# Plain f32 projections in place of three split products, and expert slots opened in the front

## The chip, the cores and the metric

The kernel runs on one core of one Trainium2 chip. The metric is the device time of one execution in microseconds, and the median of several executions is compared. The profile is one execution taken by the hardware profiler.

## The reference

One layer of a streaming encoder for 256 frames of width 2048, all in f32. A projection of the normalised input feeds two mixers of 1024 channels each, a gated causal convolution and an RWKV-7 recurrence; their joined output is projected back and added. A mixture of 32 experts (one of four groups, then two of its eight experts for each token) and a last norm follow.

```python
def reference(x, norm_mix, w_in, ..., norm_final):
    h = x
    for l in range(DEPTH):                      # DEPTH = 1
        u = rms_norm(h, norm_mix[l])
        proj = u @ w_in[l]                      # 2048 -> 2*1024 + 3*1024 + 288
        conv_val = proj[..., :D_CONV]
        conv_gate = proj[..., D_CONV:2 * D_CONV]
        rwkv_cols = proj[..., 2 * D_CONV:]
        y_conv = conformer_conv(conv_val, conv_gate, conv_dw[l], ...)
        y_rwkv = rwkv7_time_mix(rwkv_cols, shift_mu[l], ...)
        mixed = jnp.concatenate([y_conv, y_rwkv], axis=-1)
        h = h + mixed @ w_out[l]                # 2048 -> 2048
        v = rms_norm(h, norm_ffn[l])
        h = h + hierarchical_moe(v, router_group_w[l], ..., expert_w_down[l])
    return rms_norm(h, norm_final)
```

An expert is `(silu(v @ w_gate) * (v @ w_up)) @ w_down` with 2048 x 512, 2048 x 512 and 512 x 2048 weights. The expert weights are 403 MB of the 471 MB that the core moves.

## The kernel before

All is on one core, and activations stay in SBUF. Until the experts, they are held with channels on the 128 partitions and the 256 tokens along the free axis, so the tokens are the moving operand of a projection and a 128 x 128 piece of the weights the stationary one.

**Input norm (`norm_in`, L278).** The input is scaled by the norm's gain into xn, TensorE forms the LoRA columns of the projection (`w_lo`, 288 wide, L315) and the sum of squares from it, and the reciprocal root is spread over a PSUM bank `rstd`. Then y = xn * rstd is formed in eight parts and split in two: yh is the value rounded to the matmul type fp32r, written by ScalarE, and yl the rest, written by VectorE.

**Projections (`proj`, L251).** A block has 256 output columns, in two halves of 128. Its weights come by SyncE's queue in chunks of 8 x 128 rows (1 MB) into the ring of pool `ringA`, whose six slots of 8 KB a partition hold the input (two slots) and weight chunks (four). `split` (L242) makes from every four rows of 128 a high part on ScalarE and a low part on VectorE. The product is the sum of three fp32r matmuls for each 128 rows: w_h x_h, w_h x_l and w_l x_h (L273 to L275). `w_in` has 20 blocks over 16 x 128 rows. `w_out` has eight blocks, done in a pass over the first six RWKV row groups, a pass over the eight convolution row groups, and a remainder over the last two (`rest_block`, L789).

**The front's order (`front`, L712).** Convolution and RWKV "duos" alternate, each with two pairs of heads or two channel groups: c0 r0 c1 r1 c2 r2 c3, the LayerNorm, r3. An RWKV duo needs its K, R and V blocks in that order (`rwkv_duo`), and its own chain of small matmuls (`rwkv_mats`, `rwkv_inv`, `rwkv_out`) runs between the projection matmuls at a set priority. Weight loads and splits have a high priority. The order on each engine is written when the program is built, from priorities.

**Experts.** They run in pairs, 16 of them, each with 24 chunks of 1 MB. `expert_up` and `expert_down` take the weights as the moving operand in plain f32, and gate, up and down products of the two experts of a pair run side by side on the two column halves of TensorE. Chunks go round a ring of 21 slots: NA = 6 in ringA, NB = 6 in ringB (opened when RWKV's tiles are closed), ND = 3 in ringD (opened after the split room is closed), NEX = 1 in ringE, and five tiles of the pool `yp` that hold yh, yl and mix in the front. `ORDER` sets the sequence. Two more places are lent once from the accumulator's tile, as the chunks from number LENT on. `fetch` (L1092) issues the load on SyncE's queue, which executes in order and waits where a slot is not yet free.

Of the kernel before, what the change touches and what calls it, by code (L numbers as in the profile page):

```python
# [21 lines left out]
D = 2048  # L22
# [16 lines left out]
WSLOT = {4: "ylb", 5: "yla", 6: 0, 7: 1}  # L39
RING = 1024  # L40
NA, NB, ND, NEX = 6, 6, 3, 1
# [5 lines left out]
LENT = 13  # L47


def ORDER(A, B, C, D, E):  # L50
    return C[0:3] + B + A[0:2] + C[3:] + D + A[2:4] + E + A[4:]

# [12 lines left out]


class Parts:
    def __init__(self, tiles, n):
        self.tiles, self.n = tiles, n

    def __getitem__(self, k):
        n = self.n
        if isinstance(k, slice):
            return self.tiles[k.start // n][:, k.start % n:(k.stop - 1) % n + 1]
        return self.tiles[k // n][:, k % n]


class Block:
# [163 lines left out]
    def split(self, view):  # L242
        nc = self.nc
        hi = self.spl.tile([128, 4, 256], F32R, tag="hi", name="hi")
        lo = self.spl.tile([128, 4, 256], F32R, tag="lo", name="lo")
        hi, lo = (t[:, 0:view.shape[1], 0:view.shape[2]] for t in (hi, lo))
        nc.scalar.activation(hi, view, AF.Copy)  # L247
        nc.vector.tensor_sub(lo, view, hi.bitcast(F32))  # L248
        return hi, lo

    def proj(self, rows, k0, nk, xh, xl, x0, slot=None):  # L251
        cols = (0, 128)
        accs = [self.bank(self.pacc, [128, 256], "acc") for _ in cols]
        early, self.early = self.early, []
        for b in range(0, nk, 8):
            nb = min(8, nk - b)
            if not early:
                with self.tc.high_priority(offset=2000):
                    c = self.chunk(rows[:, k0 + b:k0 + b + nb], slot)
            for g in range(0, nb, 4):  # L260
                ng = min(4, nb - g)
                with self.tc.high_priority(offset=2000):
                    if early:
                        c, cut = early.pop(0)
                    else:
                        cut = None
                    hi, lo = cut or self.split(c[:, g:g + ng, :])
                for ci, cc in enumerate(cols):
                    for j in range(ng):
                        kt = b + g + j  # L270
                        w_h, w_l = hi[:, j, cc:cc + 128], lo[:, j, cc:cc + 128]
                        x_h, x_l = (x[x0 + kt] for x in (xh, xl))
                        self.mm(accs[ci], w_h, x_h, start=kt == 0, stop=False)  # L273
                        self.mm(accs[ci], w_h, x_l, start=False, stop=False)
                        self.mm(accs[ci], w_l, x_h, start=False, stop=kt == nk - 1)  # L275
        return accs

    def norm_in(self):  # L278
# [13 lines left out]
        xn = [self.rwkv_parts(i, F32, "y") for i in range(2)]  # L292
# [3 lines left out]
        for g in range(4):  # L296
            sq = self.spl.tile([128, 4, 256], F32, tag="hi" if g % 2 else "lo", name="nsq")
            A.activation(sq, x(4 * g, 4), AF.Square)
            for k in range(4 * g, 4 * g + 4):
                o, c = xn[k // 8][k % 8], self.nmix_s[:, k:k + 1]  # L300
# [19 lines left out]
        for step in PSTART:  # L320
            n = int(step[1:] or 0)
            for i in range(2):
                ts = slice(128 * i, 128 * i + 128)
                if step[0] == "l":
                    ordered(la[i], xn[n // 8][n % 8][:, ts], wl[n], start=n == 0, stop=n == 15)
# [3 lines left out]
                else:  # L329
# [5 lines left out]
        yh, yl = (Parts([self.ypool.tile([128, 8, 256], F32R, tag=n + h, name=n + h) for h in "ab"], 8)  # L335
                  for n in ("yh", "yl"))
        tmp = self.ypool.tile([128, 4, 2, 256], F32, tag="mix", name="ytmp")
        first = [self.chunk(self.w_in[DC // 256][:, 8 * b:8 * b + 8]) for b in range(2)]
        self.early = []
        for g in range(8):  # L340
            s = slice(2 * g, 2 * g + 2)
# [4 lines left out]
            if g % 2:  # L346
                c = first[g // 4]
                k = 2 * (g - 1) % 8
                self.early.append((c, self.split(c[:, k:k + 4]) if g < 6 else None))
        self.yh, self.yl = yh, yl  # L350
        self.la, self.rs = la, rs

    def rwkv_parts(self, i, dt, name):
        return Parts([self.mp.tile([128, n, 256], dt, tag=f"m{i}{h}", name=f"{name}{i}{h}")
                      for h, n in (("a", 6), ("b", 2))], 6)

    def w_in_cols(self, c0):
        return self.proj(self.w_in[c0 // 256], 0, 16, self.yh, self.yl, 0)

    def shift(self, ps, mu, omu, out):  # L360
        nc = self.nc
        nc.scalar.activation(out, ps, AF.Copy, scale=omu)
        nc.vector.scalar_tensor_tensor(out[:, 1:256], ps[:, 0:255], mu, out[:, 1:256],
                                       op0=OP.mult, op1=OP.add)

# [57 lines left out]
    def rwkv_k(self, s, kps):  # L423
# [4 lines left out]
        self.shift(kps, self.pcol("mu_k", p), self.omu[:, 1, p:p + 1], ks)  # L428
# [23 lines left out]
        s.update(AR=AR, bt=bt, kt=kt, ks=ks)  # L452

# [122 lines left out]
    def rwkv_out(self, s):  # L576
# [63 lines left out]
        V.tensor_mul(ys, ys, g)  # L640
        self.hilo(ys, self.mr[0][p], self.mr[1][p])
        self.tap(f"mix{p}", ys)
# [18 lines left out]
    def conv_norm(self):  # L661
# [11 lines left out]
        rstd = self.ypool.tile([128, 256], F32, tag="yha", name="lnr")  # L673
        A.activation(rstd, var, AF.Sqrt, bias=self.c_ln, scale=1.0 / DC)
        V.reciprocal(rstd, rstd)
        for j in range(8):
            c = self.mix[:, j]
            V.tensor_mul(c, c, rstd)
# [4 lines left out]

    def hilo(self, src, hi, lo):
        self.nc.scalar.activation(hi, src, AF.Copy)
        self.nc.vector.tensor_sub(lo, src, hi.bitcast(F32))
# [25 lines left out]
    def front(self):  # L712
        tc, nc = self.tc, self.nc
        self.mix = self.ypool.tile([128, 8, 256], F32, tag="mix", name="mix")
        self.mr = [self.rwkv_parts(i, F32R, "mr") for i in range(2)]
        V = nc.vector
        with tc.issue_after(self.gate_y.ins), tc.issue_after(self.gate_h.ins):
# [20 lines left out]
    def mix_out(self):  # L738
        m = self.ap.tile([128, 2, 8, 256], F32R, tag="vt", name="m")
        self.mh, self.ml = ([m[:, i, j] for j in range(8)] for i in range(2))  # L740
        self.w_out_pass(8, 6, *self.mr, 0)
        for j in range(8):
            self.hilo(self.mix[:, j], self.mh[j], self.ml[j])
        self.tap("mix", self.mix)
        self.w_out_pass(0, 8, self.mh, self.ml, 0, WSLOT)
# [29 lines left out]
    def w_out_pass(self, k0, nk, xh, xl, x0, slots={}):  # L775
        for b in range(8):
            ps = self.proj(self.w_out[b], k0, nk, xh, xl, x0, slots.get(b))
# [11 lines left out]
    def rest_block(self, b):  # L789
        accs = [self.bank(self.pacc, [128, 256], "acc") for _ in range(2)]  # L790
        cs = slice(256 * b, 256 * b + 256)
        hi, lo = (t[:, b % 3] for t in self.wsp)
        with self.tc.high_priority(offset=2000):
            for k in range(2):
                self.nc.scalar.activation(hi[:, k], self.wrest[k][:, cs], AF.Copy)
                self.nc.vector.tensor_sub(lo[:, k], self.wrest[k][:, cs], hi[:, k].bitcast(F32))
        for i in range(2):
# [497 lines left out]
```

## Time and profile before

| | |
|---|---|
| median of 3 runs | 1467.24 us (1467.2 to 1469.68) |
| profiled execution, its own time | 1469.49 us |
| its span | 1467.7 us |
| TensorE busy | 1399.4 us (95%), 8738 matmul records |
| VectorE busy | 648.2 us (44%) |
| ScalarE busy | 415.5 us (28%) |
| moved by DMA | 471.48 MB, mean 321 GB/s |
| granted TensorE clock, mean | 0.989 |

In the profile PE is TensorE's matmuls, PEld its weight loads, DVE VectorE, ACT ScalarE, POOL GpSimd, SP SyncE, and SPq SyncE's queue. A plain f32 matmul leaves two matmul records, an fp32r one leaves one; both are printed as f32. Matmuls overlap in the pipeline, so the step from one record's start to the next one's is their cost, not the duration of one, and a busy PE can still have slack. L219 is the line of the helper `mm`, which issues most matmuls; they are told apart by the names of their operands, out<-in: acc is a projection's accumulator, g and u the experts' gate and up products, y their down product, gt the gathering of tokens, mm the RWKV chain.

### The profile page before, as it was taken

The page shows a single profiled execution, that of the slowest core. Times are in us where ns is not written, and L with a number is a line of the kernel's source. Part 1 is how long each engine was busy: PE and PEld are TensorE (multiplying, and loading weights), DVE is VectorE, ACT ScalarE, POOL GpSimd, SP SyncE. Part 2 cuts the span into 40 slices and gives each one's busy share as a digit, 9 for nine tenths or more (in the row PEclk, how much of TensorE's full clock was granted, in tenths as well). Part 3 has the DMA queues.
Part 4 walks back from the last instruction along what each step waited for, and adds up shares of the span by engine and source line. Part 5 has one row for each costly group of instructions (what it writes and reads, how often), then busy time and mean ns, then how long its engine had stood idle before and what let it go on. Part 6 is the DMA issues. An engine that isn't in the chain of part 4 may idle for free.

```text
span 1467.7 us, 21322 instructions
## 1 busy us (share of the span) xinstructions
PE 1399.4 (95%) x8738; PEld 854.7 (58%) x8738; DVE 648.2 (44%) x1323; ACT 415.5 (28%) x770; POOL 34.3 (2%) x66
## 2 busy tenths in 40 slices
PE   8999999999999979999999999999999998999995
PEld 6989988888899944344344344344344343443432
DVE  6996977968867432232232232232132221312313
ACT  6657666676695420000000000000010000000103
POOL 5000000000000000000000000000000000000000
PEclk9999999999999989999999999999999999999997
DMA  8442432422548777999999999999999999999994
GB/s 300 158 149 96 142 119 90 152 96 89 180 138 333 301 273 324 424 423 427 424 424 425 424 424 423 426 424 424 425 424 424 424 425 424 423 427 424 423 422 151
DMA packets 68678, 471.48 MB, mean 321 GB/s; under 512 B 7984, under 2 KB 10096, under 8 KB 13280
## 3 DMA queue, kind: packets, MB, share of 16 engines
q1 hardware_dynamic: 67344, 467.96, 78.5%
q0 software_dynamic: 1088, 2.09, 0.6%
q8 instruction: 71, 1.16, 0.3%
q14 instruction: 31, 0.25, 0.0%
q10 hardware_dynamic: 144, 0.01, 0.0%
HBM read 467.93 MB, written 2.10 MB: 320 GB/s over the span
## 4 chain that ended last, share of the span: by engine, by line
PE 58%; DMA 26%; DVE 12%; ACT 3%; issue 1%; SPq 0%; ACTq 0%; DVEq 0%
DMA w<-in_w_up_dram 18%; PE acc L219 12%; PE y L219 10%; PE g L219 9%; PE u L219 9%; DMA w<-in_w_down_dram 8%; PE mm L219 7%; PE gt L219 6%; DVE lo L248 3%; PE cb L219 3%; DVE mix L659 2%; DVE MB L496 1%; PE acc L315 1%; ACT hi L247 1%; PE cn L219 1%
## 5 line engine op out<-in xcount | busy, mean ns | idle before, releaser
L219 PE MATMUL u<-w,xe 128*64 128x512 f32 x1016 | 244.1, 593 | 10.3 <-DMA w<-in_w_up_dram 10.2
L219 PE MATMUL g<-w,xe 128*64 128x512 f32 x1016 | 241.4, 597 | 10.4 <-DMA w<-in_w_gate_dram 7.9
L219 PE MATMUL y<-w,hT 128*64 128x512 f32 (+1 forms) x1040 | 232.2, 594 | 0.7 <-ACT hT L1038 0.7
L1056 DVE TENSOR_TENSOR acc<-acc,cb 128x512 f32<-128x512 f32 (+1 forms) x122 | 80.9, 674 | 208.4 <-PE cb L219 208.4
L219 PEld LDWEIGHTS u<-w,xe 128*64 128x64 f32 x1016 | 76.1, 137 | 159.8 <-issue 136.1
L1030 DVE TENSOR_TENSOR hid<-sg,u 128x256 f32<-128x256 f32 x32 | 19.7, 614 | 319.0 <-PE u L219 319.0
L219 PEld LDWEIGHTS g<-w,xe 128*64 128x64 f32 x1016 | 71.8, 137 | 148.4 <-issue 127.6
L219 PEld LDWEIGHTS y<-w,hT 128*64 128x64 f32 x1040 | 70.6, 137 | 134.1 <-issue 118.1
L248 DVE TENSOR_TENSOR lo<-w,hi 128x1024 fp32r<-128x1024 f32 x108 | 127.6, 1182 | 39.8 <-ACT hi L247 27.1
L1026 ACT ACTIVATE sg<-g 128x512 f32<-128x512 f32 x16 | 9.6, 597 | 462.2 <-PE g L219 462.2
L219 PE MATMUL gt<-S,vt 128*128 128x128 f32 x1024 | 127.8, 282 | 6.7 <-DVE xe L977 5.2
L219 PEld LDWEIGHTS gt<-S,vt 128*128 128x128 f32 x1024 | 122.4, 196 | 15.7 <-DVE xe L977 8.7
L247 ACT ACTIVATE hi<-w 128x1024 fp32r<-128x1024 f32 x108 | 110.6, 1025 | 43.6 <-PE acc L219 40.4
L1069 ACT ACTIVATE yh<-y,gate 128x512 fp32r<-128x512 f32 (+1 forms) x65 | 44.3, 682 | 250.4 <-PE y L219 250.4
L659 DVE SCALAR_TENSOR_TENSOR mix<-UP,dw_s,mix 128x256 f32<-128x256 f32 x240 | 104.1, 479 | 2.8 <-ACT mix L657 2.5
L219 PE MATMUL acc<-yha,hi 128*128 128x256 f32 x320 | 91.6, 286 | 1.1 <-ACT sg L646 0.6
L219 PE MATMUL acc<-yhb,lo 128*128 128x256 f32 x320 | 92.0, 287 | 0.0
L219 PE MATMUL acc<-yla,hi 128*128 128x256 f32 x320 | 91.7, 287 | 0.0
L219 PE MATMUL acc<-ylb,hi 128*128 128x256 f32 x320 | 91.3, 285 | 0.0
L219 PE MATMUL acc<-yha,lo 128*128 128x256 f32 x320 | 90.9, 285 | 0.0
L219 PE MATMUL acc<-yhb,hi 128*128 128x256 f32 x320 | 90.4, 282 | 0.0
L977 DVE TENSOR_TENSOR xe<-gt,nffnp_s 128x512 f32<-128x512 f32 (+1 forms) x65 | 44.4, 684 | 88.8 <-PE gt L219 88.8
(356 smaller groups left out, 1913.3 us busy)
## 6 DMA issues: line engine op xcount, KB each, us to landing
w<-in_w_gate_dram SPq DMA_DIRECT2D x127, 1024.0 KB, 19.6
w<-in_w_up_dram SPq DMA_DIRECT2D x127, 1024.0 KB, 19.6
w<-in_w_down_dram SPq DMA_DIRECT2D x126, 1024.0 KB, 19.6
w<-in_w_in_dram SPq DMA_DIRECT2D x40, 1024.0 KB, 5.0
w<-in_w_out_dram SPq DMA_DIRECT2D x8, 768.0 KB, 4.4
w<-in_w_out_dram SPq DMA_DIRECT2D x6, 1024.0 KB, 5.1
xT_s<-in_xT_dram SPq DMA_DIRECT2D x4, 512.0 KB, 6.5
wlast<-in_w_out_dram SPq DMA_DIRECT2D x2, 1024.0 KB, 6.9
```

Of the source, the lines that this page charges most:

```text
L219: self.nc.tensor.matmul(*a, **k)
L247: nc.scalar.activation(hi, view, AF.Copy)
L248: nc.vector.tensor_sub(lo, view, hi.bitcast(F32))
L315: m = nc.tensor.matmul(*a, **k)
L496: V.copy_predicated(MB[:, 2 * h + c], self.mkP.rearrange("p a b -> p (a b)"), P12[h])
L659: V.scalar_tensor_tensor(c, u, d, c, op0=OP.mult, op1=OP.add)
L977: self.nc.vector.tensor_mul(xe[:, a:a + n], ps, self.nffnp_s[:, k0:k0 + n, None].to_broadcast([128, n, 128]))
L1026: A.activation(sg, gp, AF.Silu)
L1030: V.tensor_mul(hid, *(t.rearrange("s (p f) -> s f p", f=4)[:, f:f + 2] for t in (sg, up)))
L1056: V.tensor_add(self.acc[:, i, c0:c0 + w], (self.vt if first else self.acc)[:, i, c0:c0 + w], cb)
L1069: A.activation(yh, yp, AF.Copy, scale=gate)
```

## The change

`proj` takes the activations and the weights as they are: one plain f32 matmul for each 128 rows in place of three fp32r ones. With that `split`, `hilo`, `Parts` and the low tiles go; y is formed in place in xn, in the tiles yha and yhb; the norm's squares lie in yla and ylb; the mixers' outputs are read as they are (mr and mix). `conv_norm` keeps its reciprocal root in PSUM. The room of the splits, pool `spl`, is gone, and ring D gets four slots (ring E goes) and is opened at the very start. The expert ring begins with yla, ylb and ring D. The first six expert fetches wait, by a semaphore, for the K shift of duos 0, 1 and 2, two each. The second w_out pass takes the ring for blocks 4 and 5 instead of yla and ylb.

```diff
-WSLOT = {4: "ylb", 5: "yla", 6: 0, 7: 1}
+WSLOT = {6: 0, 7: 1}
-NA, NB, ND, NEX = 6, 6, 3, 1
+NA, NB, ND = 6, 6, 4
+EARLY = 6
-LENT = 13
-def ORDER(A, B, C, D, E):
-    return C[0:3] + B + A[0:2] + C[3:] + D + A[2:4] + E + A[4:]
+LENT = 14
+def ORDER(A, B, C, D):
+    return C[0:2] + D + C[2:4] + B + C[4:] + A
...
+    def proj(self, rows, k0, nk, x, x0, slot=None):
...
-            for g in range(0, nb, 4):
...
-                for ci, cc in enumerate(cols):
-                    for j in range(ng):
-                        kt = b + g + j
-                        w_h, w_l = hi[:, j, cc:cc + 128], lo[:, j, cc:cc + 128]
-                        x_h, x_l = (x[x0 + kt] for x in (xh, xl))
-                        self.mm(accs[ci], w_h, x_h, start=kt == 0, stop=False)
-                        self.mm(accs[ci], w_h, x_l, start=False, stop=False)
-                        self.mm(accs[ci], w_l, x_h, start=False, stop=kt == nk - 1)
+            for ci, cc in enumerate(cols):
+                for j in range(nb):
+                    self.mm(accs[ci], c[:, j, cc:cc + 128], x[x0 + b + j], start=b + j == 0, stop=b + j == nk - 1)
...
-        xn = [self.rwkv_parts(i, F32, "y") for i in range(2)]
+        xn = [self.ypool.tile([128, 8, 256], F32, tag=t, name="y") for t in ("yha", "yhb")]
+        sqt = [self.ypool.tile([128, 2, 4, 256], F32, tag=t, name="nsq") for t in ("yla", "ylb")]
...
-            y = tmp[:, g % 4]
-            V.tensor_mul(y, xn[g // 4][2 * (g % 4):2 * (g % 4) + 2], rstd[:, None, :].to_broadcast([128, 2, 256]))
-            self.gate_h = A.activation(yh[s], y, AF.Copy)
-            self.gate_y = V.tensor_sub(yl[s], y, yh[s].bitcast(F32))
...
+            y = xn[g // 4][:, 2 * (g % 4):2 * (g % 4) + 2]
+            self.gate_y = V.tensor_mul(y, y, rstd[:, None, :].to_broadcast([128, 2, 256]))
+        self.y = [xn[k // 8][:, k % 8] for k in range(16)]
...
-        rstd = self.ypool.tile([128, 256], F32, tag="yha", name="lnr")
-        A.activation(rstd, var, AF.Sqrt, bias=self.c_ln, scale=1.0 / DC)
-        V.reciprocal(rstd, rstd)
+        A.activation(var, var, AF.Sqrt, bias=self.c_ln, scale=1.0 / DC)
+        V.reciprocal(var, var)
...
         for i in range(2):
-            self.rwkv_k(ss[i], ps[i])
+            gate = self.rwkv_k(ss[i], ps[i])
+        if len(self.gates) < EARLY:
+            self.gates += [gate] * 2
...
-                for w, x in ((hi, 0), (hi, 1), (lo, 0)):
-                    self.mm(accs[i], w[:, k, c], self.mr[x][6 + k], ...)
+                self.mm(accs[i], self.wrest[k][:, c:c + 128], self.mr[:, 6 + k], start=k == 0, stop=k == 1)
...
+        gate = self.gates.pop(0) if self.gates else None
+        return self.fetch(self.slot(rings, "w"), which, e, q, gate)
...
-        self.nc.sync.dma_start(v, src)
+        d = self.nc.sync.dma_start(v, src)
+        if gate is not None:
+            self.after(d, gate)
...
             self.ring = E(P("ringA", NA))
+            rd = E(P("ringD", 1))
...
-                    sp = fw.enter_context(ExitStack())
-                    self.spl = sp.enter_context(P("spl", 3, "right"))
...
-                    C = [(self.ypool, n) for n in ("yhb", "yha", "mix", "ylb", "yla")]
+                    C = [(self.ypool, n) for n in ("yla", "ylb", "yha", "yhb", "mix")]
```

## Rows read from the trace of the kernel before

**Rows 1.** Table by stretches: length, each engine's busy us, clock, DMA share, GB/s.

```profile
27.00:447.00 420.00, 407.17 (x3558) 372.58 (x3558) 349.18 (x705) 288.51 (x549) 21.68 (x42) 1.00 0.39 132
447.00:519.00 72.00, 72.00 (x615) 71.92 (x614) 42.57 (x79) 33.65 (x63) 0.00 (x0) 1.00 0.84 331
526.00:592.00 66.00, 62.71 (x323) 30.55 (x323) 17.00 (x50) 5.54 (x9) 0.00 (x0) 0.96 0.75 302
592.00:977.00 385.00, 382.57 (x1947) 168.37 (x1946) 99.44 (x197) 27.62 (x42) 0.00 (x0) 1.00 1.01 424
977.00:1391.00 414.00, 393.26 (x1948) 170.35 (x1946) 99.94 (x198) 27.68 (x43) 0.52 (x1) 1.00 1.01 424
```

**Rows 2.** Waits of TensorE, 27 to 447 us: total us, times, longest.

```profile
PE mm L219 <- DVE DT L498: 6.9, 8, 1.4
PE mm L219 <- ACT sq L430: 2.5, 5, 1.0
PE mm L219 <- ACT EP L536: 0.9, 5, 0.3
PE acc L219 <- ACT sg L646: 0.6, 1, 0.6
PE acc L219 <- DVE ks L363: 0.5, 2, 0.3
```

**Rows 3.** The chain of waits, expert stage: start us, us, what.

```profile
592.15 3.58 PE g L219 x16
...
647.16 3.58 PE g L219 x16
...
985.47 19.70 DMA w<-in_w_up_dram
1005.23 21.31 DMA w<-in_w_down_dram
1026.61 19.58 DMA w<-in_w_up_dram
```

**Rows 4.** Waits of TensorE, 526 us to the end: total us, times, longest.

```profile
PE u L219 <- DMA w<-in_w_up_dram: 10.2, 8, 1.3
PE g L219 <- DMA w<-in_w_gate_dram: 7.9, 7, 1.4
```

**Rows 5.** Timeline and waits, SyncE's queue and TensorE, the experts' beginning.

```profile
376.53 0.42 SPq L1095 DMA_DIRECT2D w<-in_w_gate_dram  x1
...
517.11 2.98 SPq L1095 DMA_DIRECT2D w<-in_w_down_dram  x3
...
526.05 3.75 PE L219 MATMUL gt<-S,vt 128*128 128x128 f32 x16 [0.98 <-DVE S L948]
...
533.99 0.33 SPq L1095 DMA_DIRECT2D w<-in_w_down_dram  x1
...
SPq L1095 <- PE g L219: 19.4, 2, 13.9
```

**Rows 6.** Plain f32 products: timeline, its group (mean ns), the chain of waits.

```profile
19.55 5.98 PE L315 MATMUL acc<-w,y1a 128*128 128x288 f32 x24
...
L315 PE MATMUL acc<-w,y1a 128*128 128x288 f32 x24 | 6.0, 406 | 0.0
...
378.33 1.73 PE cn L219 x8
```

**Rows 7.** Split products in the chain of waits: start us, us, what.

```profile
29.12 9.07 PE acc L219 x80
...
447.67 53.09 PE acc L219 x448
```

**Rows 8.** One of six groups of w_in's split products, by form.

```profile
L219 PE MATMUL acc<-yha,hi 128*128 128x256 f32 x320 | 91.6, 286 | 1.1 <-ACT sg L646 0.6 <-DVE ks L363 0.5
```

**Rows 9.** The splits' groups: busy us, mean ns, idle before and its cause.

```profile
L248 DVE TENSOR_TENSOR lo<-w,hi 128x1024 fp32r<-128x1024 f32 x108 | 127.6, 1182 | 39.8 <-ACT hi L247 27.1 <-PE acc L219 9.2 <-PE mm L219 3.3
L247 ACT ACTIVATE hi<-w 128x1024 fp32r<-128x1024 f32 x108 | 110.6, 1025 | 43.6 <-PE acc L219 40.4 <-issue 1.5 <-ACT bv L465 0.7
```

**Rows 10.** Timeline of TensorE around a piece of RWKV's chain.

```profile
300.84 0.39 PE L219 MATMUL mm<-dd,at 128*128 128x128 f16 x4
301.04 0.36 PE L219 MATMUL acc<-yha,hi 128*128 128x256 f32 x1
301.24 0.28 PE L219 MATMUL acc<-yla,hi 128*128 128x256 f32 x1
301.36 0.28 PE L219 MATMUL acc<-yha,lo 128*128 128x256 f32 x1
```

**Rows 11.** Loads of w_in (KB, us to landing), and SyncE's wait.

```profile
w<-in_w_in_dram SPq DMA_DIRECT2D x40, 1024.0 KB, 5.0
...
SPq L239 <- DVE lo L248: 250.4, 29, 13.6
```

More of the change, by code (lines that the diff above doesn't have):

```diff
@@ L240, in chunk @@
         return v
[L242 to L251, printed above, removed]
+    def proj(self, rows, k0, nk, x, x0, slot=None):
         cols = (0, 128)
@@ L334, in norm_in @@
                     ordered(rstd[:, ts], self.ones, dg[:, i], start=True, stop=True)
[L335 to L339, printed above, removed]
-        for g in range(8):
-            s = slice(2 * g, 2 * g + 2)
-            y = tmp[:, g % 4]
-            V.tensor_mul(y, xn[g // 4][2 * (g % 4):2 * (g % 4) + 2], rstd[:, None, :].to_broadcast([128, 2, 256]))
-            self.gate_h = A.activation(yh[s], y, AF.Copy)
-            self.gate_y = V.tensor_sub(yl[s], y, yh[s].bitcast(F32))
[L346 to L350, printed above, removed]
+        self.early = [self.chunk(self.w_in[DC // 256][:, 8 * b:8 * b + 8]) for b in range(2)]
+        for g in range(8):
+            y = xn[g // 4][:, 2 * (g % 4):2 * (g % 4) + 2]
+            self.gate_y = V.tensor_mul(y, y, rstd[:, None, :].to_broadcast([128, 2, 256]))
+        self.y = [xn[k // 8][:, k % 8] for k in range(16)]
         self.la, self.rs = la, rs
-    def rwkv_parts(self, i, dt, name):
-        return Parts([self.mp.tile([128, n, 256], dt, tag=f"m{i}{h}", name=f"{name}{i}{h}")
-                      for h, n in (("a", 6), ("b", 2))], 6)
     def w_in_cols(self, c0):
-        return self.proj(self.w_in[c0 // 256], 0, 16, self.yh, self.yl, 0)
+        return self.proj(self.w_in[c0 // 256], 0, 16, self.y, 0)
     def shift(self, ps, mu, omu, out):
         nc = self.nc
-        nc.scalar.activation(out, ps, AF.Copy, scale=omu)
+        a = nc.scalar.activation(out, ps, AF.Copy, scale=omu)
         nc.vector.scalar_tensor_tensor(out[:, 1:256], ps[:, 0:255], mu, out[:, 1:256],
                                        op0=OP.mult, op1=OP.add)
+        return a
     def tt(self, name, shape=(128, 256), dt=F32):
@@ L427, in rwkv_k @@
         ks = self.lg("ks")
-        self.shift(kps, self.pcol("mu_k", p), self.omu[:, 1, p:p + 1], ks)
+        gate = self.shift(kps, self.pcol("mu_k", p), self.omu[:, 1, p:p + 1], ks)
         sq = self.tt("sq")
@@ L452, in rwkv_k @@
         s.update(AR=AR, bt=bt, kt=kt, ks=ks)
+        return gate
     def rwkv_r(self, s, rps):
@@ L714, in front @@
         self.mix = self.ypool.tile([128, 8, 256], F32, tag="mix", name="mix")
-        self.mr = [self.rwkv_parts(i, F32R, "mr") for i in range(2)]
+        self.mr = self.mp.tile([128, 8, 256], F32, name="mr")
         V = nc.vector
-        with tc.issue_after(self.gate_y.ins), tc.issue_after(self.gate_h.ins):
+        with tc.issue_after(self.gate_y.ins):
             V.tensor_copy(self.id16[:, 0], self.ident)
@@ L738, in mix_out @@
     def mix_out(self):
[L739 to L743, printed above, removed]
+        self.w_out_pass(8, 6, [self.mr[:, j] for j in range(8)], 0)
         self.tap("mix", self.mix)
-        self.w_out_pass(0, 8, self.mh, self.ml, 0, WSLOT)
+        self.w_out_pass(0, 8, [self.mix[:, j] for j in range(8)], 0, WSLOT)
         with self.tc.high_priority(offset=2000):
@@ L773, in conv_duo, with w_out_pass @@
             self.conv_taps((2 * d, 2 * d + 1), ps, sg)
[L775 removed]
+    def w_out_pass(self, k0, nk, x, x0, slots={}):
         for b in range(8):
[L777 removed]
+            ps = self.proj(self.w_out[b], k0, nk, x, x0, slots.get(b))
             for i in range(2):
@@ L790, in rest_block @@
         accs = [self.bank(self.pacc, [128, 256], "acc") for _ in range(2)]
[L791 to L793 removed]
+        for i in range(2):
+            c = 256 * b + 128 * i
             for k in range(2):
[L795 to L802 removed]
+                self.mm(accs[i], self.wrest[k][:, c:c + 128], self.mr[:, 6 + k], start=k == 0, stop=k == 1)
         return accs
@@ L807, in w_out_rest @@
         V, A = nc.vector, nc.scalar
-        self.wsp = [self.mp.tile([128, 3, 2, 256], F32R, tag=t, name=t) for t in ("m0a", "m1a")]
         self.vt = self.ap.tile([128, 2, D], F32, tag="vt", name="vt")
@@ L1084, in expert_chunk @@
             return self.fetch(self.lent.pop(0), which, e, q)
-        return self.fetch(self.slot(rings, "w"), which, e, q)
+        gate = self.gates.pop(0) if self.gates else None
+        return self.fetch(self.slot(rings, "w"), which, e, q, gate)
     def slot(self, rings, name):
@@ L1090, in slot, with fetch @@
         return pool.tile([128, 2048], F32, tag=tag, name=name)
-    def fetch(self, c, which, e, q):
+    def fetch(self, c, which, e, q, gate=None):
         src = self.wsrc(which, e, q)
         v = c[:, 0:4 * src.shape[2]].rearrange("p (a b) -> p a b", a=4)
-        self.nc.sync.dma_start(v, src)
+        d = self.nc.sync.dma_start(v, src)
+        if gate is not None:
+            self.after(d, gate)
         return v
```

46 lines of the change are left out of this document (11 added, 35 removed).

## The prediction, made before the changed kernel was built or run

> **What bounds the kernel now.** I read the table by stretches first [rows 1]. Three numbers decide in it: how much of a stretch TensorE is without a matmul, what the DMA engines move, and the granted clock. [...] From 592 us the DMA moves 424 GB/s without a break. VectorE is the second busiest in the front, 349 of 420 us, but TensorE waits for other engines 6.9, 2.5, 0.9, 0.6 and 0.5 us there, 11.4 us in all [rows 2]. So the front is TensorE's.
>
> The expert stage has two laws, which the chain of waits shows [rows 3]. From 592 us it is made of matmuls, and a pair of experts takes 647.16 - 592.15 = 55.0 us. From 985 us it is made of DMA landings of about 19.7 us, three to a pair, 59 us: TensorE consumes faster than weights come, and the store that it started with is used up. TensorE's waits for weights are 10.2 and 7.9 us, in small pieces [rows 4].
>
> The third view, decisive for the freed room, is SyncE's queue [rows 5]. The kernel has 21 slots for expert weights and two lent ones. The first fetch leaves at 376.53 us, the 23rd in the group that begins at 517.11 us, before the experts' first gather at 526.05 us. The 24th stands at 533.99 us: it waited 13.9 us, until a first expert matmul had freed a slot. So the experts start with all 23 places filled or asked for, and the DMA idles after that for want of room (302 GB/s from 526 to 592 us [rows 1]), not because it began late.
>
> **The change part by part.** All sums are made against the profiled execution: 1469.49 us, span 1467.7, 2.25 us over the median of 1467.24.
>
> *One plain product for three.* A plain f32 call leaves two matmul records: the twelve calls of the LoRA product on the six parts of y1a are 24 records, of 288 columns, and take 5.98 us; less the last record's own 0.41, that is 5.57 / 23 = 242 ns from record to record, and 256/288 of it is 215 ns. The mean product of the convolution norm, 256 columns wide, gives the same: 8 records in 1.73 us, 216 each [rows 6]. A plain projection matmul thus costs 2 x 215.5 = 431 ns. The stationary operand changes from call to call in the LoRA rows too, so its loads are in that figure.
>
> A split product is one record. 80 in a row take 9.07 us, 113.4 ns each; 448 in a row 53.09 us, 118.5 ns each [rows 7]. Three are 340 to 356 ns. The new form is therefore dearer on TensorE by 75 to 91 ns for each triple.
>
> How many: w_in has 20 column blocks x 16 x 2 = 640 calls ([rows 8]: 320 records for each of six products, 1920 = 3 x 640). The first pass of w_out has 8 x 6 x 2 = 96, the second 128, the remainder 32. The 736 of the first two run in the 27-447 stretch, where both paces occur; I take 115 ns, or 345 a triple: 736 x 86 = 63.3 us. The 160 others run at the slower pace: 160 x 75.5 = 12.1 us. Sum +75.4 us. With 113.4 ns for the 736 it is 736 x 90.8 + 12.1 = 78.9; with 118.5 for all it is 67.6.
>
> *What TensorE gets back.* First, waits. ScalarE loses 108 copies of 1025 ns, VectorE 108 subtractions of 1182 ns [rows 9], some 239 us of work on the two engines that RWKV's chain runs on. None of it is on the path by itself: TensorE was kept busy beside it. It can return at most the 12.8 us in which TensorE lacked a matmul. Second, restarts. After a piece of the RWKV chain the second split product starts 0.20 us after the first, against 0.12 between the next ones [rows 10]. Such steps number about 150 in the front, so at most 150 x 0.085 = 12.8 us goes with them; part of it is no loss, since the first product starts early, and plain products follow f32 or f16 work at their own pace in the rows of 256 columns. The bounds are 0 and 26 us. I take 15: longer projection matmuls and idler helpers cover more of the chain, but the order on TensorE is written at build time and will keep some waits.
>
> *Start and norms.* y is now formed in place, so its later parts wait for the LoRA products that read the unscaled values. These end about when the first projection starts anyway, and that one needs the first half only. The LayerNorm scale stays in PSUM: a few operations of under 2 us. The remainder of w_out loses its own splits; TensorE is full there. Together 0, within 2 us.
>
> *Slots in the front.* Four ring-D slots and the two former low-part tiles, yla and ylb, are open from the start or from the end of the input norm; six fetches are gated on the K shifts of duos 0 to 2. yha and yhb follow the last input projection. Eight chunks of 1.049 MB, 2.47 us each at 424 GB/s, move out of the stretch 447-526. But the number of slots stays 21 plus two, all were asked for before the experts began [rows 5], and from there a chunk is fetched when one is consumed, as before. A store of the same size carries TensorE equally far, to its 985 us. Gain 0; between 0 and -8 x 2.47 = -20 us if the store was in truth short. It delays nothing visible: the w_in loads land in 5.0 us, and four ring slots hold two column blocks, 2 x 32 x 0.431 = 27.6 us of matmuls.
>
> *Sum.* 75.4 - 15 + 0 = +60 us, all before the experts start (526 to about 586 us); everything behind is shifted whole. 1469.5 + 60 = 1529.5 for a profile, 1527 for the median. Bounds of the terms: 67.6 - 26 = +42, and 78.9 - 0 = +79, that is 1509 to 1546.
>
> **The rivals.**
>
> *A. The early slots pay.* If the expert stage's DMA limit is set by when fetching starts, eight chunks count: 1527 - 20 = 1507. For it: from 985 us landings are the chain [rows 3]. Against: the fetch at 533.99 waited for a matmul, not for the DMA [rows 5], and the pairs from 592 us are made of matmuls alone [rows 3].
>
> *B. The gated fetches block SyncE's queue.* A fetch that waits for ScalarE's K shift (L428) holds every w_in load queued behind it, and TensorE starves once the 27.6 us of stored blocks less the 5.0 of a landing are gone, 22.6 us. SyncE's queue is indeed one that blocks: it waited 250.4 us for the splits' subtractions in the front [rows 11]. The price of a gate passed 10 us after that cover is 10 us, once in each of three duos: 1557. Against: a gate belongs to the block that runs just before the loads behind it.
>
> *C. Faster: a record of plain f32 streams once.* If one record took a single stream of 256 columns, as a split product does, a call would cost 2 x 113.4 = 227 ns instead of 345. The place is the front's TensorE, and it decides from under 345 ns a call. 736 x 118 + 160 x 128 = 107 us less, 1360 us, if the RWKV chain on VectorE (349 us, less some 130 of splits) can follow. Against it stand the 242 and 216 ns [rows 6]; nothing in the trace is for it. [...]
>
> *D. The front is VectorE's, so the splits were the price.* Then the front would shrink with 128 us less there. TensorE's 407.2 of 420 us rules it out beyond the 12.8 us already counted.
>
> **How the numbers follow.** Forecast (1512 to 1546 around 1527): 0.75. A: 0.07. B and other new waits of TensorE: 0.13. C: 0.03. The remaining 0.02 is a cancellation that I can't name. The range holds the forecast, A, and B up to about half of its price: 1506 to 1552. A change under 0.2%, 3 us, can't be told from none for this kernel; the only cases that end faster are C and half of the unnamed, 0.03, same 0.01, slower 0.96.
>
> **What would show it.** Right: products acc of 1792 records at 215 to 216 ns from record to record; first expert matmul near 586 us with expert weights landed long before; pairs of 55 us, then landings of 19.7 us in threes; DMA rate in the front up by the early chunks and nothing gained for it. SyncE's first fetch that waits on an expert matmul shows that the slots were full again. A is right if the part from the first gather to the end is shorter than before's 1467.7 - 526 = 942 us by ten or more. B is right if TensorE waits for w_in landings. C is right if records stand 110 ns apart. Wrong altogether if TensorE's waits in the front grow, or if the first gather comes before 560 us.

## The result, and the profile of the changed kernel

The changed kernel takes 1546.64 us (median; 1545.65 to 1548.09) where the kernel before took 1467.22 in four runs: 1.054 times as long [1.0523, 1.0561]. The forecast was 1527 with a range of 1506 to 1552. The direction and most of the size are right; 20 us are not in the sum.

The profiled execution took 1546.83 us, 77.3 more than that of before. One event divides the difference: the experts' first gather starts at 600.00 us in place of 526.05 [rows 5]. So 73.95 us arise ahead of it, 3.4 behind it.

The table by stretches of the changed kernel follows. Columns are start:end, length, busy us of TensorE, its weight loads, VectorE, ScalarE and GpSimd, then granted clock, DMA share and GB/s. The last line is a stretch of the landing-bound part.

```profile
27.00:447.00 420.00, 414.97 (x2569) 338.92 (x2568) 226.12 (x552) 173.36 (x373) 15.85 (x35) 1.00 0.38 128
447.00:519.00 72.00, 62.34 (x322) 49.79 (x320) 21.82 (x51) 25.66 (x60) 0.00 (x0) 0.91 0.35 124
600.00:666.00 66.00, 62.76 (x323) 30.52 (x323) 16.82 (x50) 5.54 (x9) 0.00 (x0) 0.96 0.74 301
666.00:1051.00 385.00, 382.58 (x1946) 168.19 (x1945) 99.36 (x196) 27.35 (x42) 0.00 (x0) 1.00 1.01 422
1095.00:1435.00 340.00, 320.72 (x1570) 136.53 (x1566) 80.68 (x158) 22.50 (x34) 0.51 (x1) 1.00 1.01 422
```

Beside [rows 1]: from 27 to 447 us VectorE has 123 us less to do and ScalarE 115, and TensorE is as full as it was, lacking a matmul for 5.0 us instead of 420.00 - 407.17 = 12.8. The second line is the surprise. In the same stretch before, TensorE was full; here 9.7 of 72 us have no matmul, and the granted clock is 0.91, a mean over the two values that this trace has, 1.00 and 0.50 (1.00 from 487 to 491 us, 0.50 from 514 to 516.4). In the expert stage the rate is 422 GB/s where it was 424 and, in the landing-bound part of before, 425.

The products themselves, from the chain of waits of the changed kernel (start us, us, what):

```profile
94.58 7.83 PE acc L209 x36
...
721.35 3.58 PE g L209 x16
...
776.41 3.58 PE g L209 x16
...
1061.63 19.58 DMA w<-in_w_up_dram
1081.28 21.22 DMA w<-in_w_down_dram
```

Thirty-six records in a row take 7.83 us; less the last one's own 0.38 (as long as its group's mean below), that is 7.45 / 35 = 213 ns from start to start. A pair of experts still takes 776.41 - 721.35 = 55.1 us, and from 1062 us the chain is landings of 19.6 and 21.2 us, as in [rows 3].

### The profile page after: what moved, and what is told of

It reads as the page before. It is cut to its first block, busy times and chain, and to the rows that moved or that the text cites. A ratio compares the mean times of both kernels' runs of the same rounds, so it can differ in the third digit from the quotient of the medians.

```text
span 1545.0 us, 19057 instructions
## 1 busy us (share of the span) xinstructions
PE 1472.1 (95%) x7842; PEld 864.8 (56%) x7842; DVE 513.6 (33%) x1171; ACT 300.0 (19%) x617; POOL 29.0 (2%) x66
## 4 chain that ended last, share of the span: by engine, by line
PE 60%; DMA 25%; DVE 13%; ACT 1%; issue 1%; SPq 0%; DVEq 0%; ACTq 0%
DMA w<-in_w_up_dram 17%; PE acc L209 16%; PE y L209 9%; PE g L209 8%; PE u L209 8%; DMA w<-in_w_down_dram 8%; PE mm L209 7%; DVE mix L616 6%; PE gt L209 5%; PE cb L209 3%; DVE MB L454 1%; PE acc L286 1%; PE cn L209 1%; DVE xe L918 1%; DMA w<-in_w_lo_dram 0%
## 5 line engine op out<-in xcount | busy, mean ns | idle before, releaser
L209 PE MATMUL acc<-y,w 128*128 128x256 f32 x1280 | 303.8, 384 | 0.0
L209 PEld LDWEIGHTS acc<-y,w 128*128 128x128 f32 x1280 | 234.9, 190 | 35.5 <-issue 7.4
L209 PE MATMUL u<-w,xe 128*64 128x512 f32 x1008 | 240.8, 593 | 13.0 <-DMA w<-in_w_up_dram 13.0
L971 DVE TENSOR_TENSOR hid<-sg,u 128x256 f32<-128x256 f32 x32 | 19.6, 612 | 322.1 <-PE u L209 322.1
L1011 DVE SCALAR_TENSOR_TENSOR yl<-y,gate,yh 128x512 fp32r<-128x512 f32 (+1 forms) x65 | 48.0, 738 | 62.1 <-ACT yh L1010 62.1
L209 PE MATMUL acc<-mr,w 128*128 128x256 f32 x256 | 63.3, 386 | 0.0
L209 PE MATMUL cb<-yh,ST 128*128 128x512 f32 (+1 forms) x130 | 57.8, 445 | 0.4 <-DVE acc L997 0.4
L209 PEld LDWEIGHTS cb<-yh,ST 128*128 128x128 f32 x130 | 24.3, 187 | 54.5 <-issue 51.1
L209 PE MATMUL cb<-yl,ST 128*128 128x512 f32 (+1 forms) x130 | 51.2, 395 | 0.3 <-DVE yl L1011 0.3
L209 PE MATMUL acc<-mix,w 128*128 128x256 f32 x192 | 44.5, 395 | 6.7 <-DVE mix L638 6.7
## 6 DMA issues: line engine op xcount, KB each, us to landing
w<-in_w_gate_dram SPq DMA_DIRECT2D x128, 1024.0 KB, 19.7
w<-in_w_up_dram SPq DMA_DIRECT2D x126, 1024.0 KB, 19.7
w<-in_w_down_dram SPq DMA_DIRECT2D x126, 1024.0 KB, 19.6
```

The lines of the kernel that those rows point to most:

```text
L209: self.nc.tensor.matmul(*a, **k)
L971: V.tensor_mul(hid, *(t.rearrange("s (p f) -> s f p", f=4)[:, f:f + 2] for t in (sg, up)))
L1011: V.scalar_tensor_tensor(yl, yp, gate, yh.bitcast(F32), op0=OP.mult, op1=OP.subtract)
```

## The experiments

The theory after this result had three parts: the product is as dear as predicted; the LayerNorm's matmuls have moved to a place where nothing covers them; and the expert weights stream a little slower. The first rival was that the rest is a longer projection, the second that the early fetches disturb the front.

### The LayerNorm put back among the projections

TensorE's timeline of the changed kernel (start us, us, engine, line, operation, out<-in, idle before and its releaser) and, below, its largest waits from 0 to 600 us that fall in this place (total us, times, longest):

```profile
483.71 8.58 PE L209 MATMUL acc<-mr,w 128*128 128x256 f32 x39
...
492.13 3.62 PE L209 MATMUL cn<-mix,ones 128*128 128x256 f32 x16
...
498.67 5.83 PE L209 MATMUL cn<-sg,ones 128*128 128x256 f32 x16 [2.92 <-DVE mix L626]
...
511.23 5.00 PE L209 MATMUL acc<-mix,w 128*128 128x256 f32 x10 [6.73 <-DVE mix L638]
```

```profile
PE acc L209 <- DVE mix L638: 6.7, 1, 6.7
...
PE cn L209 <- DVE mix L626: 2.9, 1, 2.9
```

The convolution's LayerNorm needs the mean (first group of cn), a subtraction, the variance (second group), a root and a scaling, before w_out's second pass (acc<-mix) can start. In the kernel before, the mean stood at 378 us [rows 6], between RWKV and projection work that ran while VectorE and ScalarE answered. Here all of it stands at 492 us, behind the last matmul of the first w_out pass. The two waits are 9.6 us. The granted clock is low there too, 0.76, which this stretch shows (columns as in the table by stretches):

```profile
492.00:520.00 28.00, 18.34 (x62) 13.14 (x61) 11.48 (x27) 14.56 (x27) 0.00 (x0) 0.76 0.20 75
```

The chain of waits in that place shows what TensorE waits for, one thing after the other:

```profile
503.33 0.42 ACT sg L628
...
503.76 1.28 ACT L630
...
505.54 1.78 DVE cn L631
...
509.14 1.09 ACT sg L636 x2
```

The order is set when the program is built, by a priority that places the LayerNorm NORM = -400 instructions away from where it is written. The diff does not touch that number. But 128 output columns cost 48 split matmuls before and 16 now, and the splits are gone, so 400 instructions are some three times as much work. A third of the number should bring it back:

```diff
-NORM = -400
+NORM = -133
```

> The changed kernel with one number different: the LayerNorm's priority offset is -133 instead of -400, which puts its matmuls back between those of the last RWKV duo. Theory (the LayerNorm slid behind the RWKV chain, where nothing covers its round trips; from its first matmul at 492.1 us to the end of the waits some 15 us more than its own matmuls): 1530 to 1535 us. Rival (its place does not matter, the excess over the forecast is dearer products or blocked fetches): 1545 to 1548 us.

Measured: 1531.24 us (1529.63 to 1532.98), ratio 1.0433 [1.041, 1.0455]; 15.4 us less than the changed kernel (16 by the two ratios). TensorE's timeline of this kernel, columns as above:

```profile
405.46 0.59 PE L209 MATMUL cn<-mix,ones 128*128 128x256 f32 x2
...
408.75 0.70 PE L209 MATMUL acc<-y,w 128*128 128x256 f32 x2
409.29 0.59 PE L209 MATMUL cn<-mix,ones 128*128 128x256 f32 x2
409.72 0.59 PE L209 MATMUL acc<-y,w 128*128 128x256 f32 x2
...
585.40 3.48 PE L209 MATMUL gt<-S,vt 128*128 128x128 f32 x16 [0.98 <-DVE S L889]
```

The mean's matmuls alternate with projection matmuls again, and the gather comes 14.6 us earlier. In this execution the stretch from 447 to 520 us has a matmul for 72.49 of 73 us:

```profile
447.00:520.00 73.00, 72.49 (x440) 60.49 (x439) 16.05 (x38) 23.18 (x58) 0.00 (x0) 1.00 0.59 218
```

### The same slip forced on the kernel before

If the place of the LayerNorm is the cause, it costs the same without plain products. The kernel before with the offset made larger:

```diff
-NORM = -400
+NORM = -1600
```

> The kernel before with the LayerNorm's priority offset at -1600 instead of -400, so that most of its matmuls stand behind the last RWKV chain, as in the changed kernel. Theory (a LayerNorm without cover costs 10 to 15 us): 1477 to 1482 us. Rival (its place does not matter): 1466 to 1469 us.

Measured: 1487.22 us (1484.63 to 1489.65), ratio 1.0124 [1.0102, 1.0145], 18 us more than before, and the gather at 545.7 us, 19.7 later. TensorE's waits from 430 to 480 us (total us, times, longest) are the ones seen above:

```profile
PE acc L219 <- ACT m L685: 7.6, 2, 7.2
PE cn L219 <- DVE mix L669: 3.3, 1, 3.3
```

The sign and the waits are as expected, the size is above what was written. With the norm put back in one kernel and put off in the other, its place is shown as the cause of the 15 us. How they divide between idle time and matmuls at the lower clock was not separated.

### The plain product alone, without the slots

The kernel before, with its slots and pools as they were, and one plain f32 product in the three products' place. Its moving operand is the high part, read as f32; the low parts of the activations are left out.

```diff
-self.mm(accs[ci], w_h, x_h, start=kt == 0, stop=False)
-self.mm(accs[ci], w_h, x_l, start=False, stop=False)
-self.mm(accs[ci], w_l, x_h, start=False, stop=kt == nk - 1)
+self.mm(accs[ci], c[:, j, cc:cc + 128], xh[x0 + kt].bitcast(F32), start=kt == 0, stop=kt == nk - 1)
```

> The kernel before with the plain product alone: one f32 matmul for three, no splits of the weights; rings, slots, room of the splits and the order of fetches as before. The activations are the rounded high parts, read as f32, so the low parts are left out of the product. Theory (product +75, some 15 given back, LayerNorm slid as in the changed kernel +15; slots worth 0): 1540 to 1549 us. Rival A (early slots pay 20 us in the changed kernel): 1560 to 1570 us. Rival B (gated early fetches cost the changed kernel its excess): 1525 to 1533 us.

Measured: 1543.58 us (1542.89 to 1543.82), ratio 1.0512 [1.0492, 1.0532]. The gather is at 600.5 us, as in the changed kernel, and the LayerNorm slides to the same place by itself, which this timeline shows (first and last of its matmul groups):

```profile
492.11 3.62 PE L219 MATMUL cn<-mix,ones 128*128 128x256 f32 x16
498.65 6.07 PE L219 MATMUL cn<-sg,ones 128*128 128x256 f32 x16 [2.92 <-DVE mix L658]
```

So the product, with the slide that it brings about, makes the whole loss ahead of the experts, and the early slots make none of it. Behind the gather this kernel takes 1542.1 - 600.5 = 941.6 us, exactly as before; the changed one takes 945.0. The two have the same granted clock over the span, 0.985, so the 3 us behind the gather belong to the slots.

### The early fetches held back

The changed kernel with its first eight expert fetches gated on the end of the first w_out pass, instead of six of them on the K shifts of duos 0 to 2:

```diff
-        if len(self.gates) < EARLY:
-            self.gates += [gate] * 2
...
+            if k0 and b == 7:
+                self.gates += [add] * 8
```

> The changed kernel with its first eight expert fetches held until the first pass of the output projection is over, so nothing of the expert weights comes in the front. Theory (the slots are full again when the experts start; worth 0): within 2 us of 1546.6. Rival A (early fetches pay): 1555 to 1567 us. Rival B (early fetches disturb the front): 1528 to 1540 us.

Measured: 1547.66 us (1547.35 to 1548.18), ratio 1.0542 [1.0522, 1.0562], against 1546.64 and 1.0542 for the changed kernel. SyncE's queue shows that the fetches did move, from 71.67 to 424.70 us in the changed kernel to these:

```profile
492.85 0.82 SPq L1037 DMA_DIRECT2D w<-in_w_gate_dram  x2
...
496.06 1.76 SPq L1037 DMA_DIRECT2D w<-in_w_up_dram  x2
```

Eight megabytes fetched 70 to 420 us earlier are worth at most the 1 us between the medians. The queue of the changed kernel shows why, in the same way as [rows 5]: at the experts' start its slots are full, and a fetch waits 14.0 us until the first gate product frees one (its timeline, and last its wait: total us, times, longest).

```profile
590.75 17.67 SPq L1037 DMA_DIRECT2D w<-in_w_down_dram  x4
608.52 3.34 SPq L1037 DMA_DIRECT2D w<-in_w_gate_dram  x2
...
SPq L1037 <- PE g L209: 14.0, 1, 14.0
```

### Where in SBUF a slot begins

The landings of chunks 100 to 350 come 2.495 us apart on average in the changed kernel, 2.483 in the kernel before. Sorted by slot, they fall in two kinds. Chunks for ring B, and before also for rings D and E, land 2.43 to 2.44 us after the one ahead (medians), the others 2.49; three to seven of the 250 steps are far longer, 2.6 to 4.1. In the built programs, ring B and the old rings D and E begin on a multiple of 256 bytes in each partition, and so do all their slots of 8192 bytes; the other slots begin 224 bytes past one. The change moved ring D to 224 past as well and dropped ring E, so 6 of 21 slots stand on a multiple where 10 did. Two edits test this on top of the earlier-LayerNorm kernel. The first moves 224 bytes of small tiles to the other end and pads, so that all 21 slots begin on a multiple of 256:

```diff
-        self.nffnp_s = self.per.tile([128, 16], F32, name="nffnp_s")
+        self.nffnp_s = self.perr.tile([128, 16], F32, name="nffnp_s")
...
+            self.perr = E(P("perr", 1, "right"))
...
+                    E(P("padm", 1)).tile([128, 56], F32, name="padm")
```

> The changed kernel with the LayerNorm at -133 (1531.2 us so far) and every expert slot at a start address in SBUF that is a multiple of 256 bytes; four small lasting tiles, 224 bytes in all, move to the other end of SBUF, and a pad of 224 bytes stands ahead of the route's tiles. So far only the six ringB slots start there, and 15 of 21 lie 32 bytes short of such a multiple. Theory (a chunk lands every 2.43 us in a slot on a multiple and every 2.49 us in the others; 15/21 x 0.057 x 345 chunks = 14 us): 1514 to 1521 us. Rival (the two paces come from the pool or the order of the ring, or from nothing that can be moved): 1530 to 1533 us.

The second only adds a pad of 32 bytes, `E(P("padm", 1)).tile([128, 8], F32, name="padm")`, so that no slot begins on one:

> The changed kernel with the LayerNorm at -133 and a pad of 32 bytes that puts ringB, the last six slots on a multiple of 256 bytes, 32 bytes past it, so that no slot is left on one. Theory: 6/21 x 0.057 x 345 = 5.6 us more than 1531.2, that is 1534 to 1539 us. Rival (address without effect): 1530 to 1533 us.

And the kernel before with the first edit, its products untouched:

> The kernel before with every expert slot at a start address that is a multiple of 256 bytes, by the same move of four small tiles and a pad; nothing else. So far 9 of 21 slots, ringB and ringD, start there. Theory: 12/21 x 0.057 x 345 = 11 us less, 1455 to 1461 us, faster than both kernels. Rival (address without effect): 1466 to 1470 us.

This expectation counts nine slots; ring E's one slot is the tenth, so its sum should have been 11/21 x 0.057 x 345 = 10 us.

Measured; the last two columns of lengths run from the start of the first gather, to the landing of the last expert chunk and to the end of the span, and each ratio is to the kernel before on the same chip:

| kernel | slots on a multiple | landing to landing, us | gather to last landing, us | gather to end, us | time, us | ratio to before |
|---|---|---|---|---|---|---|
| changed, LayerNorm back, all aligned | 21 | 2.470 | 912.2 | 936.5 | 1523.55 | 1.0394 [1.0377, 1.0412] |
| before, all aligned | 21 | 2.470 | 911.5 | 936.7 | 1461.98 | 0.9964 [0.995, 0.9979] |
| before | 10 | 2.483 | 916.9 | 941.6 | 1465.39 | 1 |
| changed, LayerNorm back | 6 | 2.495 | 919.4 | 942.7 | 1531.24 | 1.0433 [1.041, 1.0455] |
| changed | 6 | 2.495 | 920.6 | 945.0 | 1546.64 | 1.0542 [1.0523, 1.0561] |
| changed, LayerNorm back, none aligned | 0 | 2.512 | 925.9 | 949.5 | 1537.38 | 1.0488 [1.047, 1.0505] |

From the tables by stretches, each kernel's landing-bound part. The changed kernel with the LayerNorm back and all slots aligned:

```profile
1080.00:1420.00 340.00, 322.47 (x1585) 137.32 (x1581) 80.02 (x157) 22.39 (x34) 0.51 (x1) 1.00 1.01 427
```

The kernel before with all slots aligned:

```profile
1020.00:1360.00 340.00, 322.50 (x1582) 137.79 (x1581) 79.94 (x157) 22.35 (x34) 0.52 (x1) 1.00 1.01 427
```

The kernel before as it was:

```profile
1020.00:1360.00 340.00, 321.21 (x1574) 136.62 (x1572) 80.73 (x158) 21.81 (x33) 0.52 (x1) 1.00 1.01 425
```

The changed kernel with the LayerNorm back and no slot aligned:

```profile
1080.00:1420.00 340.00, 318.82 (x1564) 139.61 (x1558) 80.81 (x158) 22.50 (x34) 0.51 (x1) 1.00 1.01 419
```

The last figures are 427, 427, 425 and 419 GB/s; the changed kernel's, above, is 422. The order is that of the number of aligned slots in each case. On one chip, all against none is 13.8 us of time. The direction and the kernel with none were as written; the gain of full alignment was smaller, and both aligned kernels missed their ranges, by 1 to 3 us: with every slot on a multiple, a chunk lands every 2.45 us in the median instead of the 2.43 that the few aligned ones showed between slower ones. What holds the rate at 427, and why a slot's start counts, is open.

### What a product costs, counted upward and downward

To learn whether TensorE's time in the front counts in full, one of the three split products was issued twice (its term is added twice):

```diff
 self.mm(accs[ci], w_h, x_l, start=False, stop=False)
+self.mm(accs[ci], w_h, x_l, start=False, stop=False)
```

> The kernel before with a fourth split product in every triple, the high weights times the low activations once more, so that term counts twice in the sum; splits, loads and slots as before. Theory (the front is TensorE's, every ns of a projection product is a ns of the span, less some 15 us that come out of waits): 736 x 115 + 160 x 118 = 104 us, so 85 to 104 us more than before, 1552 to 1572 us; the LayerNorm's offset now reaches less far, which costs nothing. Rival (the helpers' waits leave room on TensorE): under 70 us more.

Measured: 1576.0 us (1574.13 to 1577.88), ratio 1.0751 [1.0679, 1.0822]: 107 us more, with the gather at 635.44, 109.4 later. 896 more matmuls at 113 to 119 ns are 101 to 107 us, so all of it shows and nothing is given back.

The other direction removes two of three: the high parts' product alone, the low parts' products and subtractions left out, the LayerNorm's offset cut in proportion.

```diff
-self.mm(accs[ci], w_h, x_h, start=kt == 0, stop=False)
-self.mm(accs[ci], w_h, x_l, start=False, stop=False)
-self.mm(accs[ci], w_l, x_h, start=False, stop=kt == nk - 1)
+self.mm(accs[ci], w_h, x_h, start=kt == 0, stop=kt == nk - 1)
```

> The kernel before with one split product in place of three, high weights times high activations; the two products with low parts and the splits' subtractions are left out, so the result has fp32r accuracy; the LayerNorm's offset is -133. It asks what would have become of the front if a call had cost a single stream, as the rival of a faster change supposed. Theory (TensorE's work shrinks by 2 x 115 x 736 + 2 x 118 x 160 = 207 us, but the chain of the RWKV duos, 4 x 60 to 100 us of small matmuls, copies and taps, then sets the front): 100 to 190 us less than before, 1275 to 1370 us. Rival (another engine already bounds the front): within 30 us of 1467.

Measured: 1461.09 us (1452.77 to 1467.79), ratio 0.9938 [0.9908, 0.9969]. About 200 us of TensorE's work went, and 7.7 us came back in the median; in the profiled execution, the slowest of the eight, the gather is at 523.7, 2.3 us earlier than before. The expectation was wrong by 90 us and more, and the rival's number was met. The table by stretches (columns as above) and TensorE's largest waits from 27 to 447 us in this kernel:

```profile
200.00:300.00 100.00, 76.44 (x496) 58.89 (x495) 58.53 (x138) 63.64 (x128) 3.23 (x6) 0.80 0.29 96
300.00:400.00 100.00, 70.20 (x436) 55.27 (x437) 39.30 (x91) 68.39 (x134) 3.22 (x6) 0.69 0.35 123
400.00:447.00 47.00, 30.88 (x223) 23.93 (x222) 12.93 (x19) 19.71 (x38) 0.00 (x0) 0.54 0.00 0
...
PE mm L219 <- DVE rs L457: 19.5, 6, 4.4
PE mm L219 <- ACT EP L532: 12.7, 12, 2.1
PE mm L219 <- DVE EP L524: 12.4, 17, 1.1
```

TensorE has no matmul for a quarter to a third of these stretches, and no engine is full, so the rival's reason, another engine that bounds the front, is not what these rows show. The waits are round trips of the RWKV chain with VectorE and ScalarE. The granted clock falls from stretch to stretch, 0.80, 0.69 and 0.54, the last near the lower value of the changed kernel's trace, 0.50. There what TensorE does takes longer: four records of mm<-AR,kt take 1.06 us at 407.05 us, and 0.60 at 381.39 us in the kernel before. So the front has a second limit near the first: the RWKV chains. How much of it the lower clock makes, and whether it is the chains' own or comes from the written order, is open, since the order's offsets count fewer instructions in this kernel too.

## Why the prediction was right, and where it was wrong

The result lies inside the stated range, and by luck: it is 0.6 us above the forecast's own 1512 to 1546, and the range reached further only for half the price of rival B, which did not happen. What failed is above all one term, that of the start and the norms.

*The price of the product: right.* The changed kernel's projection records are 1280 + 256 + 192 + 64 = 1792, as forecast. Its groups of products, by form (busy us, mean ns | idle before):

```profile
L209 PE MATMUL acc<-y,w 128*128 128x256 f32 x1280 | 303.8, 384 | 0.0
L209 PE MATMUL acc<-mr,w 128*128 128x256 f32 x256 | 63.3, 386 | 0.0
L209 PE MATMUL acc<-mix,w 128*128 128x256 f32 x192 | 44.5, 395 | 6.7 <-DVE mix L638 6.7
L209 PE MATMUL acc<-mix,wlast 128*128 128x256 f32 x64 | 14.0, 379 | 0.0
```

The median step from one to the next is 216 ns, where 215.5 was taken from the LoRA and norm rows [rows 6].

*What TensorE gets back: the sum right, one of its reasons wrong.* With the LayerNorm back in its place, the gather comes 585.40 - 526.05 = 59.35 us later than before; 75.4 - 59.35 leaves 16 given back where 15 was forecast. TensorE's listed waits from 27 to 447 us fall from 11.4 us [rows 2] to the 4.4 of these rows of that kernel (total us, times, longest), and 0.5 more come from there to 520 us:

```profile
PE mm L209 <- DVE Ph L369: 1.6, 2, 0.8
PE mm L209 <- DVE rs L419: 1.5, 2, 0.8
PE mm L209 <- DVE DT L456: 1.3, 8, 0.2
```

That is 6.5 of the 16. The restarts, which were to give up to 12.8, do not give it. From the last matmul of other work to the second product behind it, the medians are 231 ns before and 328 after behind full-size f16 matmuls, 334 and 432 behind f32 ones of 256 columns; over all forms it is 96 to 99 more, and the step between products itself is 100 longer (116 and 216). "Plain products follow f32 or f16 work at their own pace" was true in part. The first step between products is 216 to 218 ns behind f32 matmuls of 128 or 256 columns on the whole array, but 272 behind full-size f16 ones and 320 behind those on a part of the array. In these rows of the changed kernel's timeline (8.90 - 0.38) us over 39 steps leaves 0.31 us for the first if the others take 216 ns, and (3.62 - 0.38) / 15 is 216 ns:

```profile
378.61 0.70 PE L209 MATMUL mm<-T,wa 64*128 64x256 f32 x4
379.24 8.90 PE L209 MATMUL acc<-y,w 128*128 128x256 f32 x40
387.98 0.59 PE L209 MATMUL mm<-sq,blk 128*128 128x256 f32 x2
388.41 3.62 PE L209 MATMUL acc<-y,w 128*128 128x256 f32 x16
```

Where the 16 come from shows when all steps from one matmul record's start to the next are added up, from the first projection product to the first gather ("other" is every matmul that is not a projection product):

| steps | before | changed, LayerNorm back |
|---|---|---|
| product to product | 2371, 117.0 ns each | 1434, 215.8 ns each |
| other to product, and from this first product to the next | 49.0 us | 73.2 us |
| product to other | 166, 43.7 us | 179, 51.3 us |
| other to other | 128.8 us | 124.2 us |

At these paces 1792 records in place of 2688 cost 72.2 us and not 75.4, so 3.2 of the 16 are the price itself. Steps from a product to other work, where most of the listed waits end, were 24.3 us over the products' pace and are 12.6, so 11.6 come back; steps inside the other work give 4.6, and the restarts, 13 more of them, take 3.3.

*Start and norms, "together 0, within 2 us": wrong, by 15 us.* This is the step that failed. It priced the operations that the diff edits and not the place of those that it leaves alone. The LayerNorm's offset was left at 400 instructions while a third of the matmul instructions remained, and the norm slid behind the work that had hidden its round trips. The start was right: the first product stands at 27.2 us, before at 27.1. The prediction's own mark for "wrong altogether" was that TensorE's waits grow in the front; they did, from 492 to 511 us. The experiments with the offset move the time by -15.4 us in the changed kernel and +18 in the one before.

*Slots in the front: the reason right, the term off by 3 us.* The early fetches are worth nothing, as argued from the full slots. What was not foreseen is that moving ring D changes where its slots begin. "Everything behind is shifted whole" missed that: 945.0 us in place of 941.6 from the gather to the end.

*The sum.* 59.35 + 14.60 (the LayerNorm) + 3.39 (behind the gather) = 77.34, the difference of the two profiled executions. The first is the forecast's 60; the others are its error.

*The rivals.* A is dead: the part behind the gather grew instead of shrinking by ten, and holding the fetches back changes nothing. B is dead: TensorE has no wait for w_in's landings, and the gates held SyncE's queue for 0.3 us in all; its companion, other new waits of TensorE, is what came, by another way than was named. C's mechanism is dead, at 216 ns a record; and its price, 1360 us, was wrong as well, since its condition, that the RWKV chain can follow, does not hold in the one-product kernel: with even less TensorE work its front ends at 524 us, at least in this order. D is dead: with 123 us less on VectorE the front grew.

*Other lengths behind the gather.* The four-product kernel takes 936.9 us from the gather to the end, 4.7 less than the kernel before with the same slots. Only 1.1 of them lie ahead of the last landing, which comes 915.8 us behind the gather (916.9 before); behind it, 21.1 us remain where 24.8 did. The granted clock differs in the 75 us that end with the last landing (the kernel before, then the four-product kernel):

```profile
1367.90:1442.90 75.00, 72.77 (x326) 30.27 (x327) 16.24 (x31) 10.48 (x17) 0.00 (x0) 0.93 0.97 400
1476.26:1551.26 75.00, 72.77 (x339) 29.68 (x339) 16.84 (x30) 11.78 (x20) 0.00 (x0) 0.98 0.98 402
```

By these two clocks TensorE had (0.98 - 0.93) x 75 = 3.8 us of full speed more, the size of the 3.7; that it is the cause was not tested. If it is, the gather-to-end length holds the clock too; the slots are read better from the last landing: 915.8 to 917.5 us in the five kernels with the slots of before, 919.4 to 920.6 in the three with those of the changed kernel.

## What to carry to other kernels

When a change alters how many instructions a piece of work has, look at every schedule offset that counts instructions, also those the diff does not touch: work that was hidden may slide out from behind its cover. Price an edit of data types or products by the step between records in rows of the same form, but ask which chain becomes the limit before a large saving on the bounding engine is booked, as the one-product kernel gave back 8 us of 200. A buffer's start address belongs to a change of layout: list it for each slot of a stream that bounds a stage; aligning all of them made the kernel before 0.36% faster, the fastest version here that computes the full reference.

## What the runs showed of the hardware beyond expectation

- Loads of 8192 bytes a partition ran at 419, 422 to 423, 425 and 427 GB/s with 0, 6, 10 and 21 of 21 destination slots beginning on a multiple of 256 bytes. In a slot 224 bytes past one a chunk took about 2.5% longer than in an aligned one of the same kernel (2.49 and 2.43 us); with the last six 32 bytes past one the average went from 2.495 to 2.512, and between none and all it is 1.7% (2.512 and 2.470). Other boundaries than 256 bytes were not tried.
- Behind other matmuls the first step between plain f32 products differed with what went before: 216 to 218 ns behind f32 of 128 or 256 columns on the whole array, 272 behind full-size f16, 320 behind matmuls on a part of the array. For split products, 116 ns apart, it is 203 and 306, 203, and 222 in the same places; but the first product then starts earlier, and from the last matmul of other work to the second product the two kinds differ by 96 to 99 ns, no more than a step.
- With TensorE without a matmul for about a third of a stretch, the granted clock was 0.54 to 0.69 in the one-product kernel, and 1.00 in the same stretch of the kernel before [rows 1].
